# Sample attention that takes two buffers of keys or values at a time and gives out its four 32-column products together

## The chip, the cores and the metric

The kernel runs on one core of one Trainium2 chip. The metric is the device time of one launch in microseconds, the median of several runs. A profile of one execution shows what each engine did: TensorE (PE for its products, PEld for its weight loads), VectorE (DVE), ScalarE (ACT), GpSimd (POOL), and SyncE (SP), whose queue issues the DMAs.

## The reference

One layer of a decoder for 512 prompt tokens and 8 sample sequences of 8 new tokens, 576 tokens in all. Three token mixers (attention, S5, gated MLP) share a projection, and a SwiGLU block follows. The change lies in the attention of the sample tokens, which read a cache of 2048 earlier positions of each sequence for 8 heads of 128:

```python
def dilated_attn_sample(q, k_all, v_all, rel_bias):
    for window, d in DILATED_PATTERNS:          # (128, 1), (512, 4), (2048, 16)
        idx = W + jnp.arange(T)[:, None] - j[None, :] * d
        kg = k_all[:, idxc]
        vg = v_all[:, idxc]
        s = jnp.einsum('nthe,ntjhe->nthj', q, kg).astype(jnp.float32) * ATT_SCALE
        s = s + strided_bias(rel_bias, d, nk).T[None, None]
        ...
        p = jnp.exp(s - lse[..., None])
        outs.append(jnp.einsum('nthj,ntjhe->nthe', p.astype(vg.dtype), vg))
    return mix_by_denominators(outs, lses)
```

All data are float32.

## The kernel before

The kernel computes with features on the partitions and the 576 tokens along the rows of each tile. Its long products (the projections, the MLP) stream weights from HBM: each 512 KB piece goes to one of two raw buffers `wr`, ScalarE and VectorE split it into a high part `wh` and a low part `wl`, and TensorE runs three passes of 128x288 products over two halves of the tokens (`mm<-xah,wh`, `mm<-xal,wh`, `mm<-xah,wl`).

The order of all instructions is fixed when the program is written. A `Driver` keeps an estimated clock for each engine. `main_tile` emits the long products and calls `D.work()` after every two blocks of 128 contracted features, which is twelve products. `D.work()` steps through a list of generators (streams) for the smaller computations. Each of them emits a step when the estimated clock says that its operands are there, and then yields. So between two groups of twelve long products there stand the steps of the attention streams that the estimate found ready. Engines then run their own instructions strictly in that order.

Sample attention (`sample_all`) works on two heads at a time, four times. Keys and values arrive as 160 loads of 128x1024 elements (512 KB), 40 for each pair of heads, into six buffers `kv` (`NKV`); `kv_load` issues a load as soon as a buffer is given back, and `kv_get` hands out the oldest buffer once the estimate says it has landed.

- Scores: for each chunk `c` of 512, 256 and 512 key positions, each head `hh` and each half `n4` of the sequences, there are four products, j = 0 to 3. Product j has a stationary operand of 32 columns (`QP`) and writes partitions 32j to 32j+31 of a PSUM tile `p` (named `s` in the trace). With 512 positions a buffer holds the keys of two j, with 256 those of four.
- Output: for each of ten blocks t of 128 positions, again four products of 32 columns (`Ps`), each with 512 columns of values, into 32-partition strips of the PSUM tile `acc`. A buffer holds the values of two j.

Of the 160 buffers 144 hold two products of 512 columns and 16 hold four of 256 columns. Before the change a step of the stream takes one buffer, emits its products and yields:

```python
def kv_get():
    while not kv_in or D.ready(kv_in[0]) + 400 > D.t:
        yield
    return kv_in.pop(0)
```

The same SP queue issues all loads and stores in program order. An issue that waits, for example a load of `wr` that waits until VectorE has finished `wl`, holds up the key and value loads behind it. Every engine instruction is recorded at one helper line, L157, so groups are told apart by tile names.

Of the kernel before, what the change touches and what calls it, by code (L numbers as in the profile page):

```python
# [19 lines left out]
T = 576  # L20
# [18 lines left out]
class Driver:  # L39
    """Emits the long products and, between their steps, the steps of the shorter computations  # L40
    whose operands are expected to be there."""

# [103 lines left out]
class Eng:  # L146
    """An engine whose instructions advance the driver's estimate of its clock."""

# [51 lines left out]
class Slots:  # L200
    """Buffers handed out to the streams."""

# [17 lines left out]
def build(tc, io):  # L220
# [50 lines left out]

    # right operands in two parts (high, low): sixteen rows of all tokens, or of half the tokens
    xpools, XT = [], []
# [15 lines left out]

# [1 line left out]
    raws = Slots([wp.tile([P, 1024], F32, name="wr%d" % i) for i in range(2)])  # L291
# [39 lines left out]
    def add_winograd(key, srcs, swap):  # L331
        """the seven left operands of one level of Winograd's product, from the blocks 11, 21, 22, 12"""
        key = [key + (nm,) for nm in ("11", "21", "22", "12")]
        wsrc.extend(zip(key, srcs))
        k11, k21, k22, k12 = key
        n = srcs[0].shape[1]

        def at(k):
            return loaded[k][0][:, :n]

        def j1():
            r = split(at(k11), n)
            V.tensor_tensor(spare[0][:, :n], at(k21), at(k22), op=ALU.add)
            return r

        def j2():
            r = split(spare[0], n)
            V.tensor_tensor(at(k21), at(k11), at(k21), op=ALU.subtract)
            return r

        def j3():
            r = split(at(k12), n)
            V.tensor_tensor(at(k11), spare[0][:, :n], at(k11), op=ALU.subtract)
            return r

        def j4():
            V.tensor_tensor(at(k12), at(k12), at(k11), op=ALU.subtract)
            r = split(at(k11), n)
            raws.give(loaded.pop(k11)[0])
            return r  # L360

        def last(k):
            def f():
                r = split(at(k), n)
                raws.give(loaded.pop(k)[0])
                return r
            return f

        jobs.append((j1, [k11, k21, k22, "ok"], None))
        jobs.append((j2, [], None))  # L370
        jobs.append((j3, [k12], None))
        jobs.append((j4, [], None))
        jobs.extend((last(k), [], None) for k in ((k12, k22, k21) if swap else (k12, k21, k22)))
# [83 lines left out]
    def mm3(out, wh, wl, xh, xl, first, last):  # L457
        """out[128, 2, 288] += W^T X in three passes"""
        for n, (w, x) in enumerate(((wh, xh), (wh, xl), (wl, xh))):
            for b in range(2):  # L460
                E.matmul(out[b], lhsT=w, rhs=x[b] if isinstance(x, tuple) else x[:, b * HT:(b + 1) * HT], start=first and n == 0,
                         stop=last and n == 2)
# [9 lines left out]

# [1 line left out]
    def rsqrt_small(v, n, bufs=2):  # L474
        """v [128, n] > 0 -> 1/sqrt(v)"""
        y = small.tile([P, n], I32, name="rq_y", tag="rq_y%d" % n, bufs=bufs)
        hv = small.tile([P, n], F32, name="rq_h", tag="rq_h%d" % n, bufs=bufs)
        t = small.tile([P, n], F32, name="rq_t", tag="rq_t%d" % n, bufs=bufs)
        V.tensor_scalar(y, v.bitcast(I32), 1, None, op0=ALU.logical_shift_right)
        V.tensor_scalar(hv, v, -0.5, None, op0=ALU.mult)  # L480
        V.tensor_scalar(y, y, -1.0, float(0x5F3759DF), op0=ALU.mult, op1=ALU.add)
        yf = y.bitcast(F32)
        for _ in range(3):
            V.tensor_tensor(t, yf, yf, op=ALU.mult)
            V.tensor_tensor(t, t, hv, op=ALU.mult)
            V.scalar_tensor_tensor(yf, t, 1.5, yf, op0=ALU.add, op1=ALU.mult)
        return yf
# [29 lines left out]

    # ================= start: x, its squares, u_ssm =================
    RSt = cst.tile([P, 5], F32, name="RSt")
# [25 lines left out]

    # the tensor engine's clock rises after some microseconds of work
    V.memset(sqacc, 0.0)
# [17 lines left out]

# [1 line left out]
    class Later:  # L567
        """Instructions put down in order, given out a few at a time."""

# [13 lines left out]
    def ssm_globals():  # L583
# [20 lines left out]
        def poly(o, x, cs):  # L604
            """((cs[0] x + cs[1]) x + ...) x"""
            V_.tensor_scalar(o, x, cs[0], None, op0=ALU.mult)
# [401 lines left out]

    # K-outer product for u_ssm
    pa, pb = mm_tile(), mm_tile()  # L1010
# [74 lines left out]

    # ================= v_sgu, tokens on the partitions =================
    sgp = tc.tile_pool(name="sgp", bufs=1, side="right")
# [114 lines left out]
    def main_tile(x0, x1):  # L1202
        """one tile of 128 outputs, all tokens; operands x0 .. x1"""
        ps = mm_tile()
# [9 lines left out]

    # ================= q, k, v =================
    def dma_when(out, src):
# [24 lines left out]

    # ================= attention =================
    ppm = tc.tile_pool(name="ppm", bufs=1)
# [116 lines left out]

    def kv_get():
        while not kv_in or D.ready(kv_in[0]) + 400 > D.t:
            yield
        return kv_in.pop(0)

    qk_ready = {}

    def sample_all():
        D.add(pair_in(0))
        for pr in range(4):  # L1370
# [7 lines left out]
            for c in range(4):  # L1378
                n = (KW + [64])[c]
                p = yield from stok.take()  # L1380
                for hh in range(2):
                    for n4 in range(2):
                        first, last = hh == 0 and n4 == 0, hh == 1 and n4 == 1
                        if c < 3:
                            per = 1024 // n
                            for j0 in range(0, 4, per):
                                kt_ = yield from kv_get()
                                for j in range(j0, j0 + per):
                                    E.matmul(p[32 * j:32 * j + 32, :n], lhsT=qp[:, hh, n4, j],
                                             rhs=kt_[:, (j - j0) * n:(j - j0 + 1) * n], start=first, stop=last)  # L1390
                                kvs.give(kt_)
                                yield
                        else:
# [33 lines left out]
            for t in range(10):  # L1427
                for j0 in (0, 2):
                    v = yield from kv_get()
                    for j in (j0, j0 + 1):  # L1430
                        E.matmul(acc[32 * j:32 * j + 32], lhsT=pt[:, t, 32 * j:32 * j + 32],
                                 rhs=v[:, (j - j0) * 512:(j - j0 + 1) * 512],
                                 start=(t == 0), stop=False, skip_group_check=True)
                    kvs.give(v)
                    yield
            while not vn_ready.get(pr):
# [66 lines left out]
    def pair_in(pr):  # L1503
        """queries, new keys and values and biases of two heads' sample rows"""
        bc = sq_.tile([P, 520], F32, name="bc", tag="bc")
# [46 lines left out]
    for h, w in heads[nh:]:  # L1552
        head_tile(h, w)
    # ================= u_sgu =================
    sgu_sq = sqacc
# [58 lines left out]

    # ================= w_out =================
    zp = tc.tile_pool(name="zp", bufs=1)
# [53 lines left out]

    # ================= the attention part, residual and norm by halves of the tokens =================
    CS = (slice(0, HT), slice(HT, T))
# [6 lines left out]
    def rs_half(th, dim, sums):  # L1679
        """RS of half the tokens from the sums of squares"""  # L1680
        while max(D.ready(s) for s in sums) + 500 > D.t:
# [79 lines left out]
    def add_sums(th, q):  # L1761
        """SQ[th] += q"""
        if sq_made[th]:
# [35 lines left out]

    # ================= the first hidden units =================  # L1800
    acts, halves_done = {}, [0] * NHID
# [123 lines left out]
    for h in range(NTH, NPLAIN):  # L1925
# [11 lines left out]
        for b in range(2):  # L1937
            D.add(act_half(h, b, t[0][b], t[1][b]))
    # ================= gate and up: one level of Winograd's product =================
    def right(i):  # L1940
        """operand i of the seven products: (high, low) by k"""
        if i in (1, 5, 3):
# [88 lines left out]

# [1 line left out]
    STG = [GT[:, 2 * i:2 * i + 2].rearrange("p a t -> p (a t)") for i in range(3)]  # L2033
# [58 lines left out]

    # ================= down projection, norm, residual =================
    ypm = tc.tile_pool(name="ypm", bufs=1)
# [28 lines left out]
    def down_wino(c, j):  # L2123
# [20 lines left out]
        def release(i):  # L2144
            """room for weights of the last part"""
            if c == 2 and j == 7:
# [135 lines left out]
def _consts():  # L2282
# [13 lines left out]
    c["lncp"] = lnc(y)[None]  # L2296
    # sample rows (j, n4, hh, t)
    rows = np.arange(P)
# [110 lines left out]
```

## Time and profile before

| | |
|---|---|
| timed runs | 2609.74, 2610.73, 2611.22 us; median 2610.73 us |
| profiled execution | span 2607.6 us from its first to its last instruction |
| TensorE busy | 2522.3 us, 97% of the span |
| VectorE, ScalarE busy | 1701.4 us (65%), 1024.2 us (39%) |
| moved by DMA | 408.90 MB, mean 157 GB/s |
| mean granted TensorE clock | 0.986 |

The span of the profiled execution is all that the trace gives of its time. What a timed run holds around the span, 2610.73 - 2607.6 = 3.1 us by the median, is taken as constant. Busy time counts an engine's instructions without overlap; issues of DMAs and waits are not in it.

### The profile page before, as it was taken

To read this page: it belongs to the slowest core of one execution; us is meant where nothing else is said; L and a number is where in the kernel's file an instruction comes from. 1 tells how busy PE (TensorE), PEld (TensorE's weight loads), DVE (VectorE), ACT (ScalarE), POOL (GpSimd) and SP (SyncE) were. 2 spreads that over 40 slices of the span, in tenths; PEclk is the share of its full clock that TensorE was granted. 3 is DMA by queue.
4 is the path that set the end of the run, shared out by engine and by line. 5 is a ranking of instruction groups with operands and counts; after the bars stand their busy time and mean duration, and the time that the engine had idled before them with its cause. 6 is when DMAs were issued, how large, how long until landed. Compare 5 with 4: busy or idle time off the path is not lost.

```text
span 2607.6 us, 44069 instructions
## 1 busy us (share of the span) xinstructions
PE 2522.3 (97%) x17852; PEld 2319.3 (89%) x17852; DVE 1701.4 (65%) x2793; ACT 1024.2 (39%) x1638; POOL 6.5 (0%) x16
## 2 busy tenths in 40 slices
PE   9984999999999999999999999999999999999996
PEld 8774896666756899989999999999999999999996
DVE  8644332322223368888787778787878778787787
ACT  5432322322223235654444444444444453434344
POOL 0000000000000000000000000000000000000000
PEclk9987999999999999999999999999999999999998
DMA  6335447767777457763343333333343543534335
GB/s 189 107 70 122 109 161 255 248 235 244 259 263 267 150 173 237 256 216 118 114 129 113 109 111 111 117 111 111 113 129 114 154 141 96 179 105 139 114 118 166
DMA packets 199892, 408.90 MB, mean 157 GB/s; under 512 B 39953, under 2 KB 97185, under 8 KB 199689
## 3 DMA queue, kind: packets, MB, share of 16 engines
q1 hardware_dynamic: 199608, 405.95, 49.4%
q8 instruction: 140, 2.29, 0.4%
q14 instruction: 64, 0.52, 0.1%
q0 software_dynamic: 80, 0.15, 0.0%
HBM read 353.25 MB, written 51.59 MB: 155 GB/s over the span
## 4 chain that ended last, share of the span: by engine, by line
PE 91%; DVE 3%; SPq 2%; DMA 2%; ACT 1%; issue 1%; another core or an unknown queue 0%; DVEq 0%; ACTq 0%
PE mm L157 24%; PE X L157 22%; PE Y L157 15%; PE s L157 9%; PE W L157 8%; PE Z L157 8%; PE acc L157 4%; SPq L157 2%; DVE wl L157 1%; DVE Y L157 1%; DMA wr<-in_wgu_dram 0%; DMA kv<-in_kt_dram 0%; ACT wh L157 0%; DVE wx L157 0%; DVE st_c L157 0%
## 5 line engine op out<-in xcount | busy, mean ns | idle before, releaser
L157 DVE TENSOR_TENSOR wl<-wr,wh 128x1024 fp32r<-128x1024 f32 (+2 forms) x315 | 327.1, 1038 | 274.4 <-ACT wh L157 272.1
L157 ACT ACTIVATE wh<-wx 128x1024 fp32r<-128x1024 f32 (+2 forms) x352 | 321.4, 913 | 318.7 <-DVE wx L157 97.7
L157 ACT ACTIVATE wh<-wr 128x1024 fp32r<-128x1024 f32 (+2 forms) x315 | 286.7, 910 | 401.1 <-PE mm L157 168.2
L157 DVE TENSOR_TENSOR wl<-wx,wh 128x1024 fp32r<-128x1024 f32 (+2 forms) x352 | 366.7, 1042 | 116.0 <-ACT wh L157 112.8
L157 PE MATMUL X<-ta,wh 128*128 128x288 f32 x1792 | 400.6, 295 | 0.0
L157 PE MATMUL X<-ta,wl 128*128 128x288 f32 x1024 | 301.6, 295 | 0.5 <-DVE wl L157 0.5
L157 PEld LDWEIGHTS X<-ta,wh 128*128 128x128 f32 x1792 | 299.7, 188 | 0.0
L157 PE MATMUL Y<-ta,wh 128*128 128x288 f32 x1056 | 249.5, 296 | 0.0
L157 PE MATMUL mm<-xah,wl 128*128 128x288 f32 x832 | 188.2, 299 | 45.0 <-DVE wl L157 45.0
L157 PE MATMUL mm<-xah,wh 128*128 128x288 f32 x832 | 198.5, 311 | 3.7 <-ACT gv L157 3.7
L157 PEld LDWEIGHTS X<-ta,wl 128*128 128x128 f32 x1024 | 192.9, 188 | 0.9 <-DVE wl L157 0.7
L157 PEld LDWEIGHTS mm<-xah,wh 128*128 128x128 f32 x832 | 136.6, 192 | 60.0 <-issue 41.8
L157 PE MATMUL Y<-ta,wl 128*128 128x288 f32 x640 | 188.5, 295 | 0.1
L157 PE MATMUL mm<-xal,wh 128*128 128x288 f32 x832 | 187.2, 297 | 0.0
L157 PEld LDWEIGHTS Y<-ta,wh 128*128 128x128 f32 x1056 | 180.5, 187 | 0.0
L157 PEld LDWEIGHTS mm<-xah,wl 128*128 128x128 f32 x832 | 138.2, 191 | 45.7 <-DVE wl L157 45.7
L157 PEld LDWEIGHTS mm<-xal,wh 128*128 128x128 f32 x832 | 138.1, 191 | 0.0
L157 ACT ACTIVATE sc<-X 128x288 f32<-128x288 f32 x120 | 48.8, 407 | 217.1 <-PE X L157 216.9
L157 PE MATMUL W<-tb,wh 128*128 128x288 f32 x640 | 129.1, 296 | 0.0
L157 PEld LDWEIGHTS Y<-ta,wl 128*128 128x128 f32 x640 | 120.4, 188 | 0.3 <-DVE wl L157 0.3
L157 DVE TENSOR_TENSOR wx<-wx 128x1024 f32<-128x1024 f32 (+3 forms) x108 | 107.7, 997 | 2.6 <-DMA wx<-hd 2.2
L157 PE MATMUL mm<-xch,wh 128*128 128x288 f32 x416 | 108.0, 306 | 0.0
(437 smaller groups left out, 5849.0 us busy)
## 6 DMA issues: line engine op xcount, KB each, us to landing
wx<-in_wgu_dram SPq DMA_DIRECT2D x98, 512.0 KB
kv<-in_kt_dram SPq DMA_DIRECT2D x80, 512.0 KB
kv<-in_vc_dram SPq DMA_DIRECT2D x80, 512.0 KB
wr<-in_wgu_dram SPq DMA_DIRECT2D x74, 512.0 KB
wr<-in_wi_dram SPq DMA_DIRECT2D x56, 512.0 KB
actw<-sc SPq DMA_DIRECT2D x98, 144.0 KB
GT<-actw SPq DMA_DIRECT2D x48, 288.0 KB
wx<-in_wdw_dram SPq DMA_DIRECT2D x39, 320.0 KB
```

The lines of the kernel that those rows point to most:

```text
L157: r = f(*args, **kw)
```

## The change

`kv_get` takes a number n and waits until the oldest n buffers are loaded. For the chunks of 512 positions, and for the values, the stream takes two buffers, emits all four products j = 0 to 3 one behind the other, gives both buffers back and yields once. The chunk of 256 positions, whose four products already share a buffer, keeps its form. The number of products, of loads and of buffers stays the same. The change also removes comments and docstrings (not shown).

```diff
-    def kv_get():
-        while not kv_in or D.ready(kv_in[0]) + 400 > D.t:
-            yield
-        return kv_in.pop(0)
+    def kv_get(n):
+
+        while len(kv_in) < n or max(D.ready(t) for t in kv_in[:n]) + 400 > D.t:
+            yield
+        r = kv_in[:n]
+        del kv_in[:n]
+        return r
...
-                            for j0 in range(0, 4, per):
-                                kt_ = yield from kv_get()
-                                for j in range(j0, j0 + per):
-                                    E.matmul(p[32 * j:32 * j + 32, :n], lhsT=qp[:, hh, n4, j],
-                                             rhs=kt_[:, (j - j0) * n:(j - j0 + 1) * n], start=first, stop=last)
-                                kvs.give(kt_)
-                                yield
+                            kts = yield from kv_get(4 // per)
+                            for j in range(4):
+                                E.matmul(p[32 * j:32 * j + 32, :n], lhsT=qp[:, hh, n4, j],
+                                         rhs=kts[j // per][:, j % per * n:(j % per + 1) * n], start=first, stop=last)
+                            kvs.give(*kts)
+                            yield
...
-                for j0 in (0, 2):
-                    v = yield from kv_get()
-                    for j in (j0, j0 + 1):
-                        E.matmul(acc[32 * j:32 * j + 32], lhsT=pt[:, t, 32 * j:32 * j + 32],
-                                 rhs=v[:, (j - j0) * 512:(j - j0 + 1) * 512],
-                                 start=(t == 0), stop=False, skip_group_check=True)
-                    kvs.give(v)
-                    yield
+                vs = yield from kv_get(2)
+                for j in range(4):
+                    E.matmul(acc[32 * j:32 * j + 32], lhsT=pt[:, t, 32 * j:32 * j + 32],
+                             rhs=vs[j // 2][:, j % 2 * 512:(j % 2 + 1) * 512],
+                             start=(t == 0), stop=False, skip_group_check=True)
+                kvs.give(*vs)
+                yield
```

The order of the program moves with it. On TensorE, where the scores of the first two heads begin (`s_74` is the PSUM tile of the scores, `kv_2955` to `kv_2960` the six buffers, x2 two products), this stands there before:

```order
L157 MATMUL s_76<-ident,zsm 64x128 x2
L157 MATMUL s_74<-kv_2955,QP_2931 32x512 x2
L157 MATMUL mm<-xah,wh_115 128x288 x2
L157 MATMUL mm<-xal,wh_115 128x288 x2
L157 MATMUL mm<-xah,wl_116 128x288 x2
L157 MATMUL mm<-xah,wh_115 128x288 x2
L157 MATMUL mm<-xal,wh_115 128x288 x2
L157 MATMUL mm<-xah,wl_116 128x288 x2
L157 MATMUL s_74<-kv_2956,QP_2931 32x512 x2
```

and with the change, at the same place on TensorE:

```order
L157 MATMUL s_76<-ident,zsm 64x128 x2
L157 MATMUL s_74<-kv_2955,QP_2931 32x512 x2
L157 MATMUL s_74<-kv_2956,QP_2931 32x512 x2
L157 MATMUL mm<-xah,wh_115 128x288 x2
L157 MATMUL mm<-xal,wh_115 128x288 x2
L157 MATMUL mm<-xah,wl_116 128x288 x2
L157 MATMUL mm<-xah,wh_115 128x288 x2
L157 MATMUL mm<-xal,wh_115 128x288 x2
L157 MATMUL mm<-xah,wl_116 128x288 x2
L157 MATMUL s_74<-kv_2957,QP_2931 32x512 x2
L157 MATMUL s_74<-kv_2958,QP_2931 32x512 x2
```

The second buffer's products have moved ahead of six rows (twelve long products). In the whole program the 144 buffers with 512-column products stand in 138 separate places before (135 alone, two runs of two, one run of five) and in 70 after (68 runs of two, two runs of four).

In one place the old order already has two buffers next to each other, on TensorE in the output of the third pair of heads. With the semaphores that each row waits for, it reads:

```order
L157 MATMUL s_76<-ident,zsm 64x128 [waits DMAHW2_49,Activation_49]
L157 MATMUL s_76<-ident,zsm 64x128
L157 MATMUL acc<-kv_2955,Ps 32x512 [waits DMAHW1_49]
L157 MATMUL acc<-kv_2955,Ps 32x512
L157 MATMUL acc<-kv_2956,Ps 32x512 [waits DMAHW4_49]
L157 MATMUL acc<-kv_2956,Ps 32x512
L157 MATMUL s_74<-zk_2953,zq_2952 128x128 [waits DVE_49]
```

Here each buffer's first product waits for its own DMA; nothing has moved in these rows, they are the old program's.

On the SP queue, at the loads that refill the buffers of the first two heads (`wr` is a weight load, `kv` a load of keys), this stands before:

```order
L157 DMA tb<-tbd 128x512
L157 DMA wr_112<-in_wi_dram 128x1024
L157 DMA kv_2955<-in_kt_dram 128x1024
L157 DMA o_v_dram<-zs 128x576
L157 DMA wr_111<-in_wi_dram 128x1024
L157 DMA kv_2956<-in_kt_dram 128x1024
L157 DMA kv_2957<-in_kt_dram 128x1024
L157 DMA kv_2958<-in_kt_dram 128x1024
L157 DMA zq_2949<-qd 128x576
```

and with the change, at the same place on the SP queue:

```order
L157 DMA tb<-tbd 128x512
L157 DMA kv_2955<-in_kt_dram 128x1024
L157 DMA wr_112<-in_wi_dram 128x1024
L157 DMA o_v_dram<-zs 128x576
L157 DMA kv_2956<-in_kt_dram 128x1024
L157 DMA kv_2957<-in_kt_dram 128x1024
L157 DMA wr_111<-in_wi_dram 128x1024
L157 DMA kv_2958<-in_kt_dram 128x1024
L157 DMA kv_2959<-in_kt_dram 128x1024
L157 DMA kv_2960<-in_kt_dram 128x1024
L157 DMA kv_2955<-in_kt_dram 128x1024
L157 DMA wr_112<-in_wi_dram 128x1024
```

The key loads have moved ahead of weight loads, and more of them stand between one weight load and the next.

## Rows read from the trace of the kernel before

**Rows 1.** The page: engine busy time, and the chain that ended last by engine.

```profile
PE 2522.3 (97%) x17852; PEld 2319.3 (89%) x17852; DVE 1701.4 (65%) x2793; ACT 1024.2 (39%) x1638; POOL 6.5 (0%) x16
...
PE 91%; DVE 3%; SPq 2%; DMA 2%; ACT 1%; issue 1%; another core or an unknown queue 0%; DVEq 0%; ACTq 0%
```

**Rows 2.** Stretch (us): engines' busy us (instructions), PEclk, DMA share, GB/s.

```profile
398.94:881.57 482.63, 479.52 (x2878) 310.72 (x2877) 134.10 (x329) 129.47 (x254) 0.00 (x0) 1.00 0.73 252
```

**Rows 3.** Groups on PE, 398.9 to 881.6: busy us, mean ns | idle, releaser.

```profile
L157 PE MATMUL acc<-kv,Ps 128*32 128x512 f32 x320 | 82.1, 605 | 0.7 <-DMA kv<-in_vc_dram 0.7
L157 PE MATMUL s<-kv,QP 128*32 128x512 f32 (+1 forms) x384 | 76.5, 533 | 1.2 <-DMA kv<-in_kt_dram 1.2
```

**Rows 4.** Timeline of PE, 398 to 406: start, us, instructions.

```profile
401.70 1.05 PE L157 MATMUL s<-kv,QP 128*32 128x512 f32 x4
402.68 0.53 PE L157 MATMUL mm<-xah,wh 128*128 128x288 f32 x2
403.05 0.42 PE L157 MATMUL mm<-xal,wh 128*128 128x288 f32 x2
...
404.11 0.42 PE L157 MATMUL mm<-xah,wl 128*128 128x288 f32 x2
404.46 1.05 PE L157 MATMUL s<-kv,QP 128*32 128x512 f32 x4
```

**Rows 5.** Timeline of PE, 423.8 to 425.9: a buffer with four 256-column products.

```profile
424.01 0.64 PE L157 MATMUL s<-kv,QP 128*32 128x256 f32 x8
424.58 0.66 PE L157 MATMUL s<-ident,zv 128*128 128x128 f32 x4
```

**Rows 6.** Timeline of PE, 736.8 to 741.1: two buffers next to each other.

```profile
736.72 0.41 PE L157 MATMUL s<-ident,zsm 128*64 128x128 f32 x2
737.06 1.06 PE L157 MATMUL acc<-kv,Ps 128*32 128x512 f32 x8
738.05 0.49 PE L157 MATMUL s<-zk,zq 128*128 128x128 f32 x2
...
738.47 1.05 PE L157 MATMUL acc<-kv,Ps 128*32 128x512 f32 x4
739.45 0.70 PE L157 MATMUL s<-zk,zq 128*128 128x256 f32 x2
```

**Rows 7.** Waits of PEld, 390 to 890: total us, times, longest us.

```profile
PEld s L157 <- DMA kv<-in_kt_dram: 4.7, 4, 1.7
...
PEld acc L157 <- DMA kv<-in_vc_dram: 2.0, 4, 0.7
```

**Rows 8.** Timeline of PE, 805 to 828: the old order's run of five buffers.

```profile
809.61 1.07 PE L157 MATMUL s<-kv,QP 128*32 128x512 f32 x8
811.49 1.05 PE L157 MATMUL s<-kv,QP 128*32 128x512 f32 x4 [0.81 <-DMA kv<-in_kt_dram]
812.77 1.05 PE L157 MATMUL s<-kv,QP 128*32 128x512 f32 x4 [0.23 <-DMA kv<-in_kt_dram]
814.00 1.05 PE L157 MATMUL s<-kv,QP 128*32 128x512 f32 x4 [0.19 <-DMA kv<-in_kt_dram]
814.99 1.10 PE L157 MATMUL s<-KN,QP 128*128 128x64 f32 x8
```

**Rows 9.** Busy time by stretch again: two of the densest for DMA.

```profile
797.00:823.00 26.00, 24.16 (x166) 16.39 (x159) 10.55 (x33) 9.55 (x14) 0.00 (x0) 1.00 1.00 354
...
750.00:780.00 30.00, 30.00 (x168) 18.48 (x166) 7.09 (x12) 7.58 (x12) 0.00 (x0) 1.00 0.80 289
```

**Rows 10.** Waits of the SP queue, 390 to 890: total us, times, longest us.

```profile
SPq L157 <- DVE wl L157: 153.8, 36, 9.3
SPq L157 <- PE s L157: 62.1, 45, 3.9
SPq L157 <- PE acc L157: 43.0, 26, 3.9
```

**Rows 11.** Chain of waits in 390 to 890: start, us, a load's issue to landing.

```profile
741.85 6.42 DMA kv<-in_vc_dram
...
805.19 8.77 DMA kv<-in_kt_dram
```

## Prediction

> **What bounds the kernel now.** I read the page first. TensorE is busy for 97% of the span and holds 91% of the chain that ended last [rows 1], so time comes off only where TensorE has less to do or waits less. Then I cut out the stretch from the first to the last product on a key or value buffer: 482.63 us, TensorE busy for 479.52 us of it, at a granted clock of 1.00 (the 2.4 GHz level), with the DMA engines busy for 0.73 of the time at 252 GB/s [rows 2]. VectorE (134.10 us) and ScalarE (129.47 us) are far from full there, so TensorE bounds this stretch, and DMA is the next in line: 0.73 x 482.63 = 352 us of transfers, which the change neither adds to nor removes. The groups of that stretch show the two kinds of product that the change touches, busy for 82.1 and 76.5 us [rows 3].
>
> **The price of one buffer.** The timeline shows it. A pair of products starts at 401.70, the next row at 402.68, the next pair at 404.46: 2.76 us a turn [rows 4]. Twelve long products stand in the turn; their rows follow each other at (404.11 - 403.05) / 4 = 0.265 us, so the six rows would take 1.59 us alone. A pair standing by itself costs 2.76 - 1.59 = 1.17 us, of which 0.98 lie between its start and the next row's start and 0.19 in the gap ahead of it and the slower start behind it.
>
> **The price of four products together.** Two rows bear on it, and both stand in the old trace. Where a buffer holds four products of 256 columns, all eight records (two for each product) take 0.57 us from start to next start (424.01 to 424.58) [rows 5]; that is near half of what two products of 512 columns take (0.98), so four strips of 32 columns run at once at that size. And where the old order happens to put two value buffers next to each other, the eight records of four 512-column products take 0.99 us (737.06 to 738.05), against 0.98 for the four records of a pair a little later (738.47 to 739.45) [rows 6]. Those four products use two buffers, and each buffer's first product carries its own DMA wait, as in the new order. So I take 1.00 + 0.19 = 1.19 us for four. The bounds are the price of one pair, 1.17 us, below, and two pairs in sequence, 2 x 0.98 + 0.19 = 2.15 us, above; I stay with 1.19 because the row is of the very same operation, size and wait.
>
> One rule of the Trainium skill speaks against this. "TensorE: Matmul & The Clock Gate", section "Measured speedup vs the span model", gives 2.38x for three column tiles of 512 columns. Three products would then take 3 / 2.38 = 1.26 times one, 0.13 more for each further tile; by that estimate a group of four takes 1.39 / 1.13 = 1.23 times a pair, about 1.21 us instead of 0.98, and the saving below would be 16 us smaller. The trace does not agree: 0.99 against 0.98 [rows 6].
>
> **The sum on TensorE.** Before, 135 buffers stand alone: 135 x 1.17 = 158.0 us. Two runs of two cost 2 x 1.19 = 2.4. The run of five takes 814.99 - 809.61 = 5.4 with its waits [rows 8], and 0.2 around it. Together 166.0 us. After, 68 runs of two buffers cost 68 x 1.19 = 80.9, and two runs of four cost 2 x (2 x 1.00 + 0.19) = 4.4: 85.3 us. The 16 buffers with 256 columns keep their form. Saved: 81 us. The long products are the same in number and stand beside nothing else on TensorE, so this comes off the path in full, unless TensorE finds its operands late.
>
> **What the wait for two buffers adds.** `kv_get(n)` itself emits nothing. But a visit now waits for two landings, and behind a late one all of TensorE stands: the next twelve or more long products, then the split of the next weights (`wl`), and then the weight load on the SP queue that waits for that split. Already before, PEld waited eight times for key or value loads, 6.7 us in all [rows 7]. In the run of five these waits are plain: 0.81, 0.23 and 0.19 us of idle time [rows 8], while the DMA engines were full (share 1.00 from 797 to 823) [rows 9]. Loads are asked for when a buffer is given back, and SP takes them in order; it waits 62.1 and 43.0 us for score and output products, and 153.8 us, up to 9.3 at a time, for `wl` [rows 10]. A load needs 6.42 or 8.77 us from issue to landing where the chain shows one [rows 11].
>
> How much later will loads be, against TensorE? Six buffers are three visits. From the release of a buffer to its next use, three pair slots disappear: 3 x (2 x 1.17 - 1.19) = 3.5 us. Part of it comes back, since the releases that SP waits for come earlier too. Each of the eight places that wait now can therefore wait up to 3.5 us longer, 28 us in all; if only the order of the loads counts, nothing is added. Places that do not wait now may begin to, so I do not go below the middle: 14 us. As a check, the stretch would then last 482.6 - 81 + 14 = 416 us with a DMA share of 352 / 416 = 0.85. That is above the 0.80 of a dense 30 us stretch in which TensorE did not wait (750 to 780) and below the 1.00 of the 26 us in which it did [rows 9], so some waiting is to be expected.
>
> **Other moves.** The SP queue's order changes (key loads pass weight loads), which costs the same number of issues; a weight load that comes behind two more key loads is covered by the 6.3 us of long products (48 x 0.132) that each half of a weight tile feeds, and if that cover failed it would show as a TensorE wait for `wh` or `wl`. Softmax steps on VectorE and ScalarE keep their work, in engines under a third full here [rows 2]. Behind the sample attention TensorE's order is the old one but for names, so that what is gained stays gained.
>
> **Forecast.** Span 2607.6 - 81 + 14 = 2540.6 us; with the 3.1 us around the span 2543.7, so 2544 us against the median of 2610.73.
>
> **Rivals.**
> - No added waits: 2610.7 - 81 = 2530 us. For it: the releases that loads wait for come earlier together with TensorE, and the DMA engines idle 27% of the stretch [rows 2]. Against: loads come in bunches behind weight loads [rows 10]. 0.13.
> - DMA holds the stretch: the share does not rise above the 0.80 that a 30 us stretch reached [rows 9], so that it lasts 352 / 0.80 = 440 us and saves 43: 2568 us. For it: the waits in rows 8 came when DMA was full. Against: 1.00 was held for 26 us. 0.17.
> - Four cost more than two: a quarter of the way from 1.00 to 1.96 us, 0.24 us more for each of 72 groups, 17 us: 2561 us. Rows 5 and 6 speak against it. 0.05. The skill's rule above would give a group of about that price.
> - The change does not do what it says: the four run two by two. Then only the gap and slow start of 72 visits are saved, 72 x (2 x 1.17 - 2.15) = 14 us: 2597 us. Against it stands the one row of eight records [rows 6]. 0.03; in a third of it waits eat the gain and nothing changes.
> - Slower: the pair is given back late, its loads queue behind a weight load's wait for `wl`, and TensorE stands at each of the 36 such waits [rows 10]. It decides from 81 / 36 = 2.25 us each; at 3 us each the time is 2610.7 - 81 + 108 = 2638 us. Against it: the same 36 waits now cost 6.7 us in all, 0.2 each [rows 7]. 0.02.
>
> **The numbers.** The forecast itself (10 to 20 us of added waits and 1 or 2 hundredths on the group's price, so 2534 to 2556) has 0.60. The range of 2526 to 2572 takes in the first three rivals and leaves out the last two and the tails, some 0.12. Faster by over 0.2% (5 us, about what a measurement of this kernel can tell from no change): 0.60 + 0.13 + 0.17 + 0.05 + 0.02 = 0.97. Within 0.2%: 0.01. Slower: 0.02.
>
> **What the profile of the changed kernel would show.** Right: rows of eight records at 1.06 us in place of two rows of four, the `acc` group's busy time down from 82.1 to about 43 us (40 x 1.06) and the score group's from 76.5 to about 44 (32 x 1.06 + 16 x 0.64); the stretch at about 416 us, its DMA share near 0.85, its clock still at 1.00; PEld's waits for key and value loads grown from 6.7 to about 20 us. Wrong: start-to-start times of a group well over 1.0 us (price of the group), waits for loads of 40 us or more (the DMA rival), or new waits on `wh` or `wl`, which this sum holds at nothing.

## The result and the profile after

The changed kernel takes 2544.14 us (median of 4 runs, 2541.18 to 2547.39) against 2610.23 us for the kernel before, measured beside it (2607.50 to 2611.22): ratio 0.9748, 95% interval 0.9734 to 0.9762. That is 66.1 us less; predicted were 2544.0 us, in a range of 2526 to 2572. The profiled execution has a span of 2543.9 us, in a run of 2545.71 us.

The page of the changed kernel, engine busy time and the chain by engine (answers to [rows 1]):

```profile
PE 2454.8 (96%) x17852; PEld 2315.6 (91%) x17852; DVE 1701.2 (67%) x2793; ACT 1023.2 (40%) x1638; POOL 6.5 (0%) x16
...
PE 89%; DVE 3%; DMA 3%; SPq 2%; ACT 1%; issue 1%; another core or an unknown queue 0%; DVEq 0%; ACTq 0%
```

As many products as before, and TensorE is busy for 2522.3 - 2454.8 = 67.5 us less: the gain is on TensorE. DMA has gone from 2% to 3% of the chain.

Windows of the changed kernel: the stretch of the key and value products (as [rows 2]), and two pieces of it.

```profile
400.11:814.72 414.61, 408.83 (x2866) 303.18 (x2865) 132.86 (x325) 128.50 (x252) 0.00 (x0) 0.99 0.83 292
456.00:464.00 8.00, 5.70 (x32) 4.43 (x31) 3.62 (x12) 1.84 (x6) 0.00 (x0) 0.79 0.44 119
756.00:764.00 8.00, 8.00 (x44) 4.36 (x45) 3.44 (x10) 3.58 (x5) 0.00 (x0) 0.79 0.81 269
```

The stretch lasts 414.61 us. It was 482.63, so it is 68.0 us shorter; the rest of the span is 4.3 us longer (2543.9 - 414.6 against 2607.6 - 482.6), in part because the stretch holds twelve records of TensorE fewer (2866 against 2878). TensorE now stands for 5.8 us of the stretch (414.61 - 408.83), against 3.1. The two short rows show something that the old stretch did not have: the granted clock falls for a moment, here to a mean of 0.79 over 8 us.

Groups of the changed kernel on PE in the stretch (as [rows 3]):

```profile
L157 PE MATMUL s<-kv,QP 128*32 128x512 f32 (+1 forms) x384 | 49.0, 544 | 1.8 <-DMA kv<-in_kt_dram 1.8
L157 PE MATMUL acc<-kv,Ps 128*32 128x512 f32 x320 | 45.8, 605 | 1.3 <-DMA kv<-in_vc_dram 1.3
```

One product's mean duration is unchanged (605 and 605 ns for values), and the group's busy time is nearly half of 82.1 and 76.5 us: the products are not shorter, more of them run at once.

Timeline of PE in the changed kernel at three places, the first being that of [rows 4]:

```profile
400.11 1.06 PE L157 MATMUL s<-kv,QP 128*32 128x512 f32 x8
401.11 0.53 PE L157 MATMUL mm<-xah,wh 128*128 128x288 f32 x2
...
402.89 1.07 PE L157 MATMUL s<-kv,QP 128*32 128x512 f32 x8
...
689.12 1.21 PE L157 MATMUL acc<-kv,Ps 128*32 128x512 f32 x8
690.64 1.05 PE L157 MATMUL acc<-kv,Ps 128*32 128x512 f32 x4 [0.31 <-DMA kv<-in_vc_dram]
691.94 1.05 PE L157 MATMUL acc<-kv,Ps 128*32 128x512 f32 x4 [0.25 <-DMA kv<-in_vc_dram]
...
753.09 1.05 PE L157 MATMUL s<-kv,QP 128*32 128x512 f32 x4
755.98 4.23 PE L157 MATMUL s<-kv,QP 128*32 128x512 f32 x12 [1.84 <-DMA kv<-in_kt_dram]
760.14 0.53 PE L157 MATMUL mm<-xah,wh 128*128 128x288 f32 x2
```

The undisturbed turn is 402.89 - 400.11 = 2.78 us with four products in it; it was 2.76 with two [rows 4]. The other two places are the two runs of four buffers. By the price of a group they should take 2.0 us each; they take 3.81 (689.12 to 692.93) and 7.05 (753.09 to 760.14). Loads come late there, and in the second the lowered clock comes on top.

Waits of the changed kernel for key and value loads on PEld, 390 to 830 us: total us, times, longest us (as [rows 7]).

```profile
PEld s L157 <- DMA kv<-in_kt_dram: 6.8, 6, 2.7
...
PEld acc L157 <- DMA kv<-in_vc_dram: 4.9, 4, 1.7
```

They have grown from 6.7 to 11.7 us. The SP queue, by contrast, waits less in sum than in [rows 10], though its longest waits for products have grown from 3.9 to 9.9 and 8.1 us:

```profile
SPq L157 <- DVE wl L157: 119.5, 33, 9.4
SPq L157 <- PE s L157: 40.8, 33, 9.9
SPq L157 <- PE acc L157: 27.4, 16, 8.1
```

### The profile page after: what moved, and what is told of

Same layout as the page of the kernel before. It is cut to its first block, busy times and chain, and to the rows that moved or that the text cites. A ratio compares the mean times of both kernels' runs of the same rounds, so it can differ in the third digit from the quotient of the medians.

```text
span 2543.9 us, 44073 instructions
## 1 busy us (share of the span) xinstructions
PE 2454.8 (96%) x17852; PEld 2315.6 (91%) x17852; DVE 1701.2 (67%) x2793; ACT 1023.2 (40%) x1638; POOL 6.5 (0%) x16
## 3 DMA queue, kind: packets, MB, share of 16 engines
q8 instruction: 140, 2.29, 0.4%
## 4 chain that ended last, share of the span: by engine, by line
PE 89%; DVE 3%; DMA 3%; SPq 2%; ACT 1%; issue 1%; another core or an unknown queue 0%; DVEq 0%; ACTq 0%
PE mm L157 24%; PE X L157 23%; PE Y L157 16%; PE W L157 8%; PE Z L157 8%; PE s L157 7%; PE acc L157 3%; SPq L157 2%; DVE wl L157 1%; DVE Y L157 1%; DMA kv<-in_vc_dram 1%; DMA wr<-in_wgu_dram 0%; DMA zv<-o_v_dram 0%; DVE st_c L157 0%; DMA wx<-hd 0%
## 5 line engine op out<-in xcount | busy, mean ns | idle before, releaser
L157 PE MATMUL mm<-xbh,wh 128*128 128x288 f32 x416 | 107.0, 304 | 0.0
```

The costliest lines, as they stand in the source:

```text
L157: r = f(*args, **kw)
```

## The experiments

The theory: the 81 us come from four 32-column products that run at once, and some 14 us of them are lost to loads that now come late. Each time below is a median beside runs of the kernel before on the same chip; the ratio to that kernel is given with its 95% interval.

**Two buffers, given out apart.** Is it the four products together, or the new order of takes and gives?

```diff
                                          rhs=kts[j // per][:, j % per * n:(j % per + 1) * n], start=first, stop=last)
-                            kvs.give(*kts)
-                            yield
+                                if j % per == per - 1:
+                                    if j == 3:
+                                        kvs.give(*kts)
+                                    yield
...
+                    if j == 1:
+                        yield
                 kvs.give(*vs)
                 yield
```

> Waits for two buffers and gives two back, as the change does, but yields between the two pairs of products, so that the four no longer stand together. If the gain is that four 32-column strips run at once, it is lost: the stretch from the first to the last key or value product is about 483 us again and the time 2611 to 2620 us (the old time, with up to 9 us of waits for two landings). If the gain comes from handling two buffers in one visit (order, releases), most of it stays: 2544 to 2565 us.

2616.68 us (2615.45 to 2617.89), ratio 1.0025 (1.0015 to 1.0035). Timeline of PE in this kernel:

```profile
398.69 1.05 PE L157 MATMUL s<-kv,QP 128*32 128x512 f32 x4
399.68 0.53 PE L157 MATMUL mm<-xah,wh 128*128 128x288 f32 x2
...
401.46 1.05 PE L157 MATMUL s<-kv,QP 128*32 128x512 f32 x4
```

A pair costs 0.99 us, as in the old kernel. Waiting for two buffers and giving two back brings nothing and costs 6.7 us; the whole gain needs the four products one behind the other. The stretch itself did not come out as expected: it lasts 507.0 us (398.69 to 905.73) in place of 483, and takes in work that stood behind it before (3059 records of TensorE against 2878). So the length of the stretch alone does not tell what a change of the order costs; the time does.

**Half the data, in the new order and in the old.** The instructions keep their order on every engine; only the size of a key or value load is halved.

```diff
-            Q.dma_start(t, a)
+            nc.sync.dma_start(t[:, :512], a[:, :512])
+            D.op("DMA", t.shape[1] * P * 4.0 / 360.0, [t], [a], 1600.0)
...
-                             rhs=vs[j // 2][:, j % 2 * 512:(j % 2 + 1) * 512],
+                             rhs=vs[j // 2][:, :512],
```

In the changed kernel:

> The changed kernel with the same order on every engine, but each key or value load moves 512 of its 1024 columns (256 KB in place of 512 KB), and all products of a buffer read those 512 columns, so that scores and values of half of the positions are left out. If the waits for key and value loads (some 15 us) come from the amount of data that the DMA engines have to move, they go and the time is 2526 to 2535 us. If they come from when the loads are issued (releases, weight loads ahead of them in the queue), it stays at 2541 to 2547 us.

2529.38 us (2529.25 to 2531.27), ratio 0.9691 (0.9675 to 0.9708): 14.8 us below the changed kernel. Its windows row of the stretch, then its groups on PE:

```profile
399.72:800.76 401.04, 400.38 (x2866) 301.01 (x2866) 132.84 (x325) 128.25 (x252) 0.00 (x0) 1.00 0.62 201
```

```profile
L157 PE MATMUL s<-kv,QP 128*32 128x512 f32 (+1 forms) x384 | 44.1, 533 | 0.0
L157 PE MATMUL acc<-kv,Ps 128*32 128x512 f32 x320 | 43.8, 604 | 0.2 <-DMA kv<-in_vc_dram 0.2
```

PEld's waits for key and value loads fall from 11.7 to 2.1 us, and the stretch from 414.6 to 401.0 us. Of these 13.6 us, 9.8 are in the two groups (busy time and idle time before them, 97.9 us together in the changed kernel and 88.1 here). Most of that lies in the two runs of four, which at the same two places of the order now take 2.23 us (682.88 to 685.11) and 1.85 us (744.90 to 746.75) in place of 3.81 and 7.05:

```profile
682.88 2.28 PE L157 MATMUL acc<-kv,Ps 128*32 128x512 f32 x16
...
744.90 1.92 PE L157 MATMUL s<-kv,QP 128*32 128x512 f32 x16
```

The rest lies nearly all at one other place, which has no key or value product in it. Timelines of PE there, of the changed kernel and then of the kernel with light loads:

```profile
456.43 0.43 PE L157 MATMUL mm<-xah,wl 128*128 128x288 f32 x2
459.16 0.90 PE L157 MATMUL s<-ident,Ss 128*128 128x128 f32 x3 [2.30 <-DVE st L157]
...
462.74 1.06 PE L157 MATMUL acc<-kv,Ps 128*32 128x512 f32 x8
```

```profile
455.22 0.43 PE L157 MATMUL mm<-xah,wl 128*128 128x288 f32 x2
455.49 0.49 PE L157 MATMUL s<-ident,Ss 128*128 128x128 f32 x3
...
457.51 1.06 PE L157 MATMUL acc<-kv,Ps 128*32 128x512 f32 x8
```

The same instructions take 6.31 us in the one and 2.29 in the other. TensorE stands for 2.30 us until VectorE has done a step of a softmax (`st`), and the long products behind it run at the lowered clock. VectorE itself was late because it waited for a load of `tb`, a table of that softmax, that was issued at 452.87 and needed 5.40 us; the first row below is of VectorE's timeline, the second of the chain of waits.

```profile
458.40 0.69 DVE L157 CUSTOM_DVE_ANT_0 Sp<-s,tb 128x512 f32<-128x512 f32 x1 [3.86 <-DMA tb<-tbd]
```

```profile
452.87 5.40 DMA tb<-tbd
```

So some 4.0 of the 13.6 us hang on a late load that is neither of keys nor of values.

In the kernel before:

> The kernel before, with the same order on every engine; each load of keys or values moves 512 of its 1024 columns, and the products of a buffer read those (scores and values of half the positions are left out). Theory: the 15 us that half the data saved in the changed kernel are waits that the change brought, since its products ask for buffers faster. The old kernel waits only some 6 to 7 us for keys and values in the whole stretch, so here half the data gains 2 to 7 us: 2603 to 2608 us. Rival: less traffic saves some 15 us in any order of the work (other loads land sooner too); then about 2595 us.

2607.33 us (2606.33 to 2609.25), ratio 0.9993 (0.9984 to 1.0003). Its windows row of the stretch:

```profile
399.67:879.41 479.74, 477.96 (x2878) 310.80 (x2878) 133.25 (x325) 129.38 (x254) 0.00 (x0) 1.00 0.52 168
```

The same lightening gives the old order 2.3 us, which is not clear of noise, and the new one 14.8. So about 12.5 us of the changed kernel's time are waits that the change brought, and they hang on the amount of data; the intervals of the four ratios leave some 6 us of doubt on that difference. And with the loads light in both, the change is worth 2607.33 - 2529.38 = 78.0 us (479.74 - 401.04 = 78.7 in the stretch): that is the price of the products and their visits alone. One row of the old order with light loads, at its run of five buffers [rows 8], will be needed below:

```profile
809.55 2.77 PE L157 MATMUL s<-kv,QP 128*32 128x512 f32 x20
812.25 1.10 PE L157 MATMUL s<-KN,QP 128*128 128x64 f32 x8
```

**One half of the change.** Values in fours, scores as before; and the other way round. Each kernel puts the old loop back in one of the two places, as in the diff of the change, with a `kv_get(1)`.

> Only the output part takes two buffers; the scores take one as before. 40 of the 72 groups of four: 40 x 1.15 = 46 us less work on TensorE, with about half of the added waits (4 to 9 us): 2568 to 2574 us. If only one of the two parts brought the gain, this would be near 2544 or near 2610 us.

> Only the scores take two buffers; the output part takes one as before. 32 of the 72 groups: 32 x 1.15 = 37 us less work on TensorE, with about half of the added waits (3 to 7 us): 2576 to 2582 us. If the two parts add up, the gains of this and of the values alone sum to 66 us or a little more.

Values alone: 2577.03 us (2574.75 to 2579.31), ratio 0.9874 (0.9859 to 0.9889). Scores alone: 2587.99 us (2587.39 to 2588.63), ratio 0.9916 (0.9901 to 0.9931). Both are slower than was expected. The gains of 33 and 22 us make 55, not 66. By the prices of the prediction 40 groups of values save 40 x (2 x 1.17 - 1.19) = 46 us and 32 of scores 37, so that each half alone loses 13 to 15 us, as much as the whole. Timelines of PE, first of the values kernel, then of the scores kernel:

```profile
783.05 1.92 PE L157 MATMUL s<-kv,QP 128*32 128x512 f32 x16
788.29 3.18 PE L157 MATMUL s<-kv,QP 128*32 128x512 f32 x8 [3.31 <-DMA kv<-in_kt_dram]
791.40 1.41 PE L157 MATMUL s<-KN,QP 128*128 128x64 f32 x8
```

```profile
780.06 1.50 PE L157 MATMUL s<-kv,QP 128*32 128x256 f32 x24
784.90 4.74 PE L157 MATMUL s<-kv,QP 128*32 128x512 f32 x16 [3.34 <-DMA kv<-in_kt_dram]
789.56 0.54 PE L157 MATMUL mm<-xah,wh 128*128 128x288 f32 x2
```

Here the program takes several buffers with no long products between them (it drains other streams at that point), so that TensorE waits for the loads: 8.35 us for 24 records and 9.50 for 40. The second row of the values kernel shows more: its eight records took 3.11 us in place of 1.0. Their second buffer was late again (the weight load waited 1.11 us for it), and behind the 3.31 us of idle time the granted clock had a mean of 0.56 in this piece. The waits thus do not grow in step with the gain, which both expectations had assumed.

**More buffers, and a more careful take.** `NKV = 7`, and `kv_get` with a margin of 2400 in place of 400 ns:

> The changed kernel with seven buffers for keys and values in place of six (the program's order moves somewhat). If the waits come from loads that are asked for too late, a load more in flight takes off a third or more of some 15 us: 2534 to 2540 us. If the DMA engines' rate makes them, it stays at 2541 to 2547 us.

> The changed kernel, where a buffer is handed out only 2400 ns after the estimate has it landed, in place of 400: the visits stand later in the order, behind more long products. If the waits only mean that products stand in the order ahead of their loads' landing, they shrink from some 15 us to 5 or less: 2532 to 2538 us. If the DMA engines are the limit of the whole stretch, nothing is won: 2541 to 2547 us.

2546.70 us (2545.46 to 2551.30), ratio 0.9759 (0.9745 to 0.9774), and 2547.38 us (2545.87 to 2548.86), ratio 0.9759 (0.9744 to 0.9773). Neither is better than the change as it stands. With the seventh buffer the waits on PEld are still 8.7 us, at a DMA share of 0.87 in the stretch; with the later take they are 7.3 us. But its stretch, which has grown to 439.3 us and holds 180 records of TensorE more, has TensorE standing for 12.2 us, 4.4 of them until a load of another tensor (`zv`). One more buffer, or a later take, does not bring the time back.

**The runs of four taken away.** The sample stream is held while the program drains others (`D.until`, `D.drain`):

```diff
     def _pass(self):
         moved = False
         for s in list(self.streams):
-            if s[2] or s[1] > self.t:
+            if s[2] or s[1] > self.t or s is self.skip:
                 continue
...
+    def hold_sample(cond):
+        D.skip = sam_s
+        D.until(cond)
+        D.skip = None
...
```

> The changed kernel, where sample attention makes no steps while the program waits for the prompt's attention or the gated MLP with no long products left to put between (two places where four buffers are now used one behind the other). If the waits there (some 7 of 11 us in the stretch) come from loads that nothing covers, they shrink and the time is 2534 to 2540 us. If the DMA engines' rate over the whole stretch sets the waits, they only move: 2542 to 2548 us.

2543.34 us (2542.18 to 2544.67), ratio 0.9744 (0.9729 to 0.9758): as the rival had it. The waits for keys and values on PEld fall to 2.5 us, but TensorE stands for more of the stretch, 7.5 us (419.42 - 411.93) against 5.8. Timeline of PE at the place of the first run, and the windows row from 685 to 695:

```profile
689.87 1.11 PE L157 MATMUL s<-ident,zv 128*128 128x128 f32 x4 [3.78 <-DMA zv<-o_v_dram]
```

```profile
685.00:695.00 10.00, 6.22 (x30) 4.58 (x29) 1.52 (x2) 3.58 (x9) 0.00 (x0) 0.83 0.96 322
```

With no values to work on, TensorE stands 3.78 us for another load (`zv`), while the DMA engines are busy for 0.96 of these 10 us. The late load has another name; the time is lost all the same.

**The price of a group, and the order of strips in it.** The values take four buffers at a time and give out eight products one behind the other: strips in the order 0123 0123, and 01 01 23 23.

```diff
-            for t in range(10):
-                vs = yield from kv_get(2)
-                for j in range(4):
+            for t0 in range(0, 10, 2):
+                vs = yield from kv_get(4)
+                for i, j in ((0, 0), (0, 1), (1, 0), (1, 1), (0, 2), (0, 3), (1, 2), (1, 3)):
+                    t = t0 + i
...
```

> The changed kernel, with the output part taking four buffers (two blocks t) in a visit: products in the order strips 0 1 2 3 of the first block, then 0 1 2 3 of the second. 20 visits fewer at 0.19 us each, but four landings to wait for: 2540 to 2552 us. It is there to be compared with the next run.

> The same eight products of the output part in a visit, the same buffers, waits and results as the run before, but in the order strips 0 1 of the first block, 0 1 of the second, 2 3 of the first, 2 3 of the second, so that only two different strips stand next to each other at a time. If four different strips run at once, each of the 20 visits costs two passes of 0.85 us more here: 34 us more than the run before, 2574 to 2586 us. If it is enough that products stand together, whatever strips they write, the two runs agree within 3 us.

Order 0123 0123: 2552.07 us (2545.92 to 2552.95), ratio 0.9769 (0.9753 to 0.9786). Order 01 01 23 23: 2550.41 us (2547.07 to 2554.05), ratio 0.9770 (0.9756 to 0.9785). The second was expected to be 34 us slower and is not. Timelines of PE, 0123 0123 first:

```profile
461.04 1.92 PE L157 MATMUL acc<-kv,Ps 128*32 128x512 f32 x16
462.90 0.53 PE L157 MATMUL mm<-xah,wh 128*128 128x288 f32 x2
```

```profile
460.62 1.94 PE L157 MATMUL acc<-kv,Ps 128*32 128x512 f32 x16
462.49 0.53 PE L157 MATMUL mm<-xah,wh 128*128 128x288 f32 x2
```

Eight products take 1.86 and 1.87 us, so that four run at once in either order. In the second, products on strips 2 and 3 stand behind all four on strips 0 and 1; since the eight at two at a time would need about four times a pair's 0.98 us, they must run beside those that stand ahead of them. The trace has it so: four records of this visit start between 460.62 and 460.65 us, and the next only at 461.07.

So the strips were then kept apart by long products: visits of four products each, on strips 0123 and 0123, or on strips 01 01 and 23 23.

```diff
...
+                for m, (i, j) in enumerate(((0, 0), (0, 1), (1, 0), (1, 1), (0, 2), (0, 3), (1, 2), (1, 3))):
...
+                    if m == 3:
+                        yield
```

> The output part takes four buffers (blocks t and t+1) and makes two visits of them, four products each: strips 0 1 2 3 of the first block, then after a yield strips 0 1 2 3 of the second. As many visits and products in a visit as in the changed kernel, but the buffers go back in fours, so that loads come later: 2544 to 2556 us. A visit takes 1.00 us. It is there to be compared with the next run.

> The same four buffers and two visits of four products, but the first visit holds strips 0 1 of both blocks and the second strips 2 3 of both. If the gain needs four different strips within reach, a visit of the output part takes 2 x 0.85 + 0.13 = 1.85 us in place of 1.00, 40 visits 34 us more than the run before: 2578 to 2590 us. If four products close together are enough, whatever strips they write, the two agree within 5 us.

Four strips in a visit: 2548.42 us (2545.97 to 2549.72), ratio 0.9762 (0.9746 to 0.9779). Two strips: 2570.53 us (2567.80 to 2571.75), ratio 0.9846 (0.9831 to 0.9861). Timelines of PE, four strips first:

```profile
459.55 1.06 PE L157 MATMUL acc<-kv,Ps 128*32 128x512 f32 x8
460.55 0.53 PE L157 MATMUL mm<-xah,wh 128*128 128x288 f32 x2
```

```profile
461.18 1.91 PE L157 MATMUL acc<-kv,Ps 128*32 128x512 f32 x8
463.02 0.53 PE L157 MATMUL mm<-xah,wh 128*128 128x288 f32 x2
```

A visit of four products costs 1.00 us on four strips and 1.84 us on two: it is the strips that make them run at once, not their number. (Two products on one strip also write the same partitions of PSUM; the two cannot be told apart here.) The whole kernel loses 22 us of the expected 40 x 0.84 = 34. The windows rows of the two stretches tell where most of the other 12 went, four strips first:

```profile
399.20:822.02 422.82, 409.97 (x2902) 309.25 (x2902) 134.81 (x330) 131.18 (x256) 0.00 (x0) 0.98 0.82 288
```

```profile
400.36:849.26 448.90, 445.93 (x2927) 318.24 (x2926) 134.30 (x329) 131.82 (x258) 0.00 (x0) 1.00 0.78 272
```

TensorE stands for 422.82 - 409.97 = 12.9 us in the first and 448.90 - 445.93 = 3.0 us in the second, which also keeps its clock at 1.00. Only 0.9 of the 12.9 us are waits for keys; 10.2 are waits for softmax steps (`st` and `Ss`), and the chain of waits leads from there to loads of `tb` and `zs` that need 4.83 to 8.64 us. With the slower TensorE these waits shrink to 1.9 us. That a slower TensorE gives the loads the time that they lack otherwise fits this, but no run varied it alone.

## Why the prediction was right

**The price of one buffer and of four products.** It held. The turn was forecast to be 0.02 us longer with four products than with two, and is (2.78 and 2.76 us). The one row of eight records in the old trace [rows 6] carried this; the kernel with light loads has the two groups at 43.8 and 44.1 us, where 43 and 44 were forecast. The rule of the Trainium skill that was weighed in the prediction ("TensorE: Matmul & The Clock Gate", section "Measured speedup vs the span model", 2.38x for three column tiles) would have given about 1.21 us for a group, by the estimate worked out there; the changed kernel's 1.00 us does not agree with it.

**The sum on TensorE.** 81 us were forecast, and 78.0 are measured between the two kernels with light loads. The forecast took the run of five at 5.4 us "with its waits"; with light loads it takes 812.25 - 809.55 = 2.70 us, which is 2.7 of the missing 3. Counted as the forecast counts, from the old kernel with its waits to the new one without, the saving is 2609.99 - 2529.38 = 80.6 us. Not all of it is products running at once. From start to next start, all rows on keys or values sum to 146.5 us in the old order and 82.2 in the new one, both with light loads: 64.3 of the 78.0 us. The other 13.7 lie around the visits, of which there are 68 fewer: 0.20 us each, where 0.19 was forecast.

**The waits for two buffers.** 14 us were forecast, and 14.8 measured against the kernel with light loads (12.5 beyond what the old order gains by them). The size was right, but in part by luck: it was the middle between 0 and 28, and the mechanism behind the 28 is not what the runs show. The eight waits did not each grow by the same delay. Half of the loss in the stretch, 6.8 of 13.6 us, sits in the two runs of four, where the program takes buffers with no long products between (1.6 and 5.2 us above what they take with light loads); 4.0 us more come from a late `tb`, which the prediction did not count; and part of both is not a wait at all but the clock behind one. So PEld's row says 11.7 us where about 20 were expected. That each half of the change alone loses as much speaks against the step by which the bound of 28 us was worked out (three pair slots fewer, for each wait): half the slots did not give half the waits.

**Two shares of the stretch.** 416 us were forecast and 414.6 measured; the DMA share of 0.83 at 292 GB/s agrees with 0.85. That the clock would stay at 1.00 was wrong. It fell behind waits of TensorE, near 459 and near 756 us. The rows from 456 to 464 and from 756 to 764 lack 0.21 of the full clock over 8 us, about 1.7 us lost each time.

**Other moves.** No product waits for `wh` or `wl` in the stretch; the moved weight loads stayed covered. The softmax steps were held at nothing because VectorE and ScalarE have room. That was wrong for one of them: it came late not for want of an engine but for want of its table `tb`, and cost the 4.0 us above. The SP queue waits less in sum; whether earlier releases are the reason was not shown.

**The rivals.** "No added waits" is the kernel with light loads, 2529.38 us where 2530 was worked out: right in price, and ruled out for the full loads. "DMA holds the stretch" (2568 us) fell: the share went past 0.80. "Four cost more" and "two by two" fell by the 1.00 us of a group. "Slower" would have needed waits above 81 us. The kernel that gives the two buffers out apart shows what a change without the strips is worth: 6.7 us lost.

**What stays open.** The late loads were tied to the amount of data, and 10.8 of the 13.6 us in the stretch to three places; why these loads are late at these places, and which other transfers hold them up, was not shown. Neither a seventh buffer, nor a later take, nor holding the stream in the drains got the 12.5 us back; a version that spreads the key and value loads over more of the program was not tried.

## What to carry to other kernels

Products that fill 32 columns of TensorE should be given out for all four strips in one visit, between two stretches of wide products: four cost what two do, 1.00 us. Before counting such a gain in full, work out the DMA share that the shortened stretch will have (352 us of transfers in 416 us here) and look in the old trace for places that already run at that rate: they show whether waits are to be expected. The waits need not fall on the loads that the change moves; here another load on the same queue, `tb`, came late too. To split a gain from the waits that it brings, halve the transfers in both kernels and keep the order: 78.0 us of products and visits and some 12.5 us of waits could be told apart by that, where undoing half of the change could not.

## What the runs showed of the hardware that was not expected

Products on other strips run beside products that stand ahead of them in the queue: eight products in the order 01 01 23 23 took 1.87 us, and 1.86 in the order 0123 0123, though strips 0 and 1 alone need 1.84 us for four. The section "The mechanism" of "TensorE: Matmul & The Clock Gate" in the Trainium skill says that products start and end in the order of the program. In strict order the third product, on strip 0 again, would hold back all behind it until the first is done: 01, then 01 beside 23, then 23, three times the half of 1.84 us, 2.8 us in all. The row of 1.87 us does not agree with that, nor do the four records that start within 0.04 us. What stands ahead of the prediction, that engines run their own instructions strictly in order, is too strong for products on different strips.

Short waits can have an aftermath. In the changed kernel the granted clock fell from the level of 2.4 GHz to that of 1.2 GHz twice, after TensorE had stood for 2.30 us (before 459.16) and for 1.84 us (before 755.98); in the kernel with values alone it had a mean of 0.56 in the 3.11 us behind a wait of 3.31 us. In the old stretch, where TensorE's longest wait was 0.81 us, it stayed at 1.00. But not every such wait is followed by it: at the same softmax step TensorE stands for 2.10 us in the kernel that holds the stream and for 2.09 us in that with visits on four strips, and the clock is 1.00 before and behind.
